# Block sums for the first FFN product: another order of the steps on the vector and activation engines

## The chip, the cores and the metric

One core of a Trainium2 chip runs the whole kernel. The metric is device microseconds of one execution, best told by the median of several runs. Engines: PE (matmul, TensorE), PEld (its weight load), DVE (VectorE), ACT (ScalarE), POOL (GpSimd) and SP, whose queue issues most DMAs. Each engine works through its own queue in order.

## The reference, cut to what matters

The block ends in a SwiGLU feed-forward network on 1024 tokens with 1024 features and DFF = 2816:

```python
h2 = rmsnorm(x, norm2_g[l]) * (1.0 + sc2) + sh2
fg, fu = jnp.split(h2 @ w_ffn_in[l], 2, axis=-1)
x = x + gt2 * ((jax.nn.silu(fg) * fu) @ w_ffn_out[l])
return rmsnorm(x, final_g)
```

The change concerns the first lines: the modulated norm `h2`, and the start of the product `h2 @ w_ffn_in`.

## The kernel before, in words

**Numbers.** Every float32 matmul is made of three matmuls on split operands. `split` (L155) writes the high part with an ACT copy (`split_hi`, L152) and the low part with a DVE subtract; `mm3` (L197) then issues high weight by high activation, high by low, low by high. A product of four 128-row tiles (128 x 512 outputs) is 12 matmuls. Where a helper records an operation, the profile gives the helper's line: nearly everything below stands under L107 or L119, so the rows are read by their tile names.

**The product.** The first FFN product is done in blocks with seven products instead of eight (`Pair`, L1144). The activations (1024 features x 1024 tokens, feature tiles in partitions) are a 2 x 2 matrix of blocks, each of KH = 4 tiles of 128 x 512: A11 (tiles 0 to 3, first half of the tokens), A12 (tiles 4 to 7, first half), A21 and A22 (second half). Sums of blocks are needed: S1 = A21 + A22, S2 = S1 - A11 (reached by two subtractions in place, L1268 and L1269), S4 = A12 - S2, S3 = A11 - A21 (in place of A21). On the weight side T1 = B12 - B11, T2 = B22 - T1, T3 = B22 - B12, T4 = B21 - T2 (`source`, L1167). `PRODUCTS` (L1146) lists the seven products with the PSUM bank (X, Y or Z) that each adds to: 0 is A11 x B11, 1 is S1 x T1, 2 is S2 x T2, 3 is S4 x B22, 4 is S3 x T3, 5 is A12 x B21, 6 is A22 x T4. `evacuate(p)` (L1216) takes what is complete out of a bank: products 0, 1 and 2 are kept by an ACT copy (`kepta`, `keptc`, `keptb`), the others end in a DVE add, and Silu on ACT for a gate pair or a DVE multiply for an up pair. Pairs alternate: even ones are gate columns, odd ones up columns, and there are NFF = 22 of them.

**Order.** `order` (L1243) begins with the first two pairs (one gate, one up) side by side, because the sums of activation blocks are being made meanwhile: product 0 of both, then 5, 1, 2, 3, 4 and 6 of both, 14 products, numbered n = 0 to 13. Then come 20 pairs with products 0 to 6 each. In the loop at L1292 step n first makes the block sums in `before[n]` (L1284), then prepares the weight block of step n + LEAD (LEAD = 6; `prepare`, L1178: a DVE subtract for a T block, then ACT high, DVE low), then issues the product and its evacuation. Ten weight blocks rotate (`weight_block`, L1247). The raw weights of a pair are loaded by `load` (L1155) through SP, into the buffers that an earlier pair frees with its T3 and T4.

**Norm and sums.** `Norm2` (L1060) has the second half of the tokens as `norms[1]`. `stat` (L1077) sums squares on PE and makes the reciprocal root on ACT (Ln, a table load, Exp); it comes after product 0 of the first pair. `apply` (L1084) scales a tile on DVE (L1087) and adds the shift on ACT (L1088). `apply1(j)` (L1258) applies the norm to tiles j and 4 + j, adds the two and splits the sum into S1. `sums` (L1265) makes S2, `sum4` (L1272) S4, and two lambdas S3 and A22, each through `act_block` (L1099), which is a split.

**Queues.** From L1280 on `in_order(True, (T, V, A))` chains the instructions of PE, DVE and ACT: each of these engines executes them in the order in which the program emits them. DMA issues on SP and POOL are not chained.

**Slots.** The four-kilobyte tiles come from 32 slots. Four S3 tiles, two hidden tiles and four A22 tiles reuse slots that become free as the sums before them are done.

Of the kernel before, what the change touches and what calls it, by code (L numbers as in the profile page):

```python
# [10 lines left out]
F32 = mybir.dt.float32  # L11
F32R = mybir.dt.float32r
AF = mybir.ActivationFunctionType
ALU = mybir.AluOpType
# [5 lines left out]
KD = D // P  # L20
KH = KD // 2
# [5 lines left out]
NFF = DFF // P  # L27
# [3 lines left out]
HB = 512  # L31
# [40 lines left out]
LEAD = 6  # L72
# [21 lines left out]
def tile_hybrid_block(ctx: ExitStack, tc: tile.TileContext, xT, vecs, cvec, lamv, relb, bsel, bmask, jrev,  # L94
# [27 lines left out]
    V, A, T, G = Engine(nc.vector), Engine(nc.scalar), Engine(nc.tensor), nc.gpsimd  # L122
# [42 lines left out]
    class Weights:  # L165
# [77 lines left out]
    def col(g, k):  # L243
        return cols[:, g * KD + k:g * KD + k + 1]
# [86 lines left out]

    small = const.tile([P, 16], F32, name="small")
    eps, eps64, heps, nlam, g08 = (small[:, i:i + 1] for i in range(5))
    G.memset(eps, EPS)
    G.memset(eps64, EPS * 2.0 ** -64)
    G.memset(heps, EPS * 2.0 ** -3)
# [27 lines left out]
    with tc.tile_pool(name="psS", bufs=2, space=bass.MemoryType.PSUM) as psS, \  # L364
# [54 lines left out]
        with tc.tile_pool(name="st", bufs=2) as st:  # L419
# [61 lines left out]
            for k in range(KD):  # L481
# [3 lines left out]
                if k in KS:  # L485
                    j = KS.index(k)
# [101 lines left out]
        for j in range(2):  # L588
# [7 lines left out]
                        op0=ALU.mult)  # L596
# [192 lines left out]
        class Norm:  # L789
# [105 lines left out]
    with tc.tile_pool(name="ps2", bufs=6, space=bass.MemoryType.PSUM) as ps2, ExitStack() as fxs:  # L895
# [69 lines left out]
        stages = dict(zip(CN, (cn.means, cn.center, squares, cn.scales, cn.finish)))  # L965
# [42 lines left out]
        for m in range(0, KD, 2):  # L1008
            i = [j[1] for j in jobs].index(m + 1) + 1
# [29 lines left out]
        x1 = []  # L1039
# [20 lines left out]
        class Norm2:  # L1060
# [20 lines left out]
                    T.matmul(st, ones, self.sq, start=False, stop=True)  # L1081
                self.r = rstd_from([st], 1.0 / D, self.last)[0]

            def apply(self, m):  # L1084

                x = x1[m][:, self.hs]
                V.scalar_tensor_tensor(out=x, in0=x, scalar=col(4, m), in1=self.r, op0=ALU.mult, op1=ALU.mult)  # L1087
                A.activation(x, x, AF.Identity, bias=col(3, m))  # L1088

        norms = [Norm2(hf) for hf in range(2)]  # L1090
        x1_d = dp.tile([KD, P, S], F32, name="x1_d")
        g_d = dp.tile([NFF, P, S], F32, name="g_d")
        acts = {}
# [50 lines left out]
        class Pair:  # L1144
# [31 lines left out]
                return b[name]  # L1176

            def prepare(self, p):  # L1178
                name = self.PRODUCTS[p][1]
                src = self.source(name)  # L1180
                w = weight_block()
                split(w[:, :HB], w[:, HB:], src)
                self.w[name] = w

            def product(self, p):
                an, bn, x = self.PRODUCTS[p]
                first = x not in self.banks
                if first:
                    self.banks[x] = bank("f" + x.lower())
                w = self.w[bn]  # L1190
                for k, a in enumerate(acts[an]):
                    ks = slice(k * P, (k + 1) * P)
                    ls = slice(HB + k * P, HB + (k + 1) * P)

                    mm3(self.banks[x], w[:, ks], w[:, ls], a[:, :HB], a[:, HB:], first and k == 0, k == KH - 1,
                        skip_group_check=not first)
# [44 lines left out]
        pairs = [Pair(i) for i in range(NFF)]  # L1241
# [5 lines left out]
        def weight_block():  # L1247
            n = nblock[0] % NWB
            nblock[0] += 1
            if n < NWB - 4:  # L1250
                return fx[0].tile([P, D], F32R, tag="wb", name="wb", bufs=NWB - 4)
            return wp.tile([P, D], F32R, tag="whi" if n % 2 else "wlo", name="wbp")
# [2 lines left out]
            if n < len(order):  # L1255
                order[n][0].prepare(order[n][1])

        def apply1(j):  # L1258
            for m in (j, KH + j):
                norms[1].apply(m)  # L1260
            t = t2("s1")
            V.tensor_tensor(out=t, in0=x1[j][:, HB:], in1=x1[KH + j][:, HB:], op=ALU.add)
            act_block("S1", j, t)

        def sums(j):  # L1265

            a11, a21, a22 = x1[j][:, :HB], x1[j][:, HB:], x1[KH + j][:, HB:]
            V.tensor_tensor(out=a21, in0=a11, in1=a21, op=ALU.subtract)  # L1268
            V.tensor_tensor(out=a11, in0=a22, in1=a21, op=ALU.subtract)  # L1269
            act_block("S2", j, a11)  # L1270

        def sum4(j):  # L1272
            a12 = x1[KH + j][:, :HB]
            V.tensor_tensor(out=a12, in0=a12, in1=x1[j][:, :HB], op=ALU.subtract)
            act_block("S4", j, a12)

        jobs += [(oc, m, Weights(w_oc[m:m + 2], D, f"oc{m}")) for m in range(0, KD, 2)]
        jobs.extend((wo, i, Weights(w_out[i % KD], D, f"wo{i}")) for i in range(2 * KD))
# [1 line left out]
        in_order(True, (T, V, A))  # L1280
        for m in range(WA[KD], KD):
            apply0(m)
        js = range(KH)
        before = {2: [(apply1, 0), (apply1, 1)], 3: [(apply1, 2)],  # L1284
                  4: [(apply1, 3)] + [(sums, j) for j in js],
                  6: [(sum4, j) for j in js],
                  8: [(lambda j: act_block("S3", j, x1[j][:, HB:]), j) for j in js],
                  10: [(lambda j: act_block("A22", j, x1[KH + j][:, HB:]), j) for j in js]}

        late = {}  # L1290
        G0 = list(range(NFF - 6, NFF))
        for n, (g, p) in enumerate(order):  # L1292
            for f, j in before.get(n, ()):
                f(j)
            nxt = n - 5 if n in (7, 8) else g.i + 2 if n >= 14 and p == 1 else NFF
            if nxt < NFF:
                pairs[nxt].load()
            prepare(n + LEAD)
            for f in late.get(n - len(order), ()):
                f()  # L1300
            g.product(p)
            if n == 0:
                norms[1].stat()
# [26 lines left out]
        x1 = []  # L1330
        for gi, grp in enumerate(groups):
            n = len(grp)
# [146 lines left out]
```

## Time and profile before

| | us |
|---|---|
| median of 3 runs | 1434.23 |
| lowest and highest | 1432.81 and 1439.95 |
| the profiled execution, its own time | 1435.16 |
| its span in the profile | 1433.4 |

In that execution PE is busy 96% of the span, DVE 69%, ACT 42%, and the mean granted PE clock is 0.979. Times of rows are microseconds from the span's start; a timeline row has start, duration, engine, line, operation, output<-input and a count, and in brackets the idle time before it with the releaser. A row with x4 is four instructions merged, and its duration runs from the first start to the last end.

### The profile page before, as it was taken

The page shows a single profiled execution, that of the slowest core. Times are in us where ns is not written, and L with a number is a line of the kernel's source. Part 1 is how long each engine was busy: PE and PEld are TensorE (multiplying, and loading weights), DVE is VectorE, ACT ScalarE, POOL GpSimd, SP SyncE. Part 2 cuts the span into 40 slices and gives each one's busy share as a digit, 9 for nine tenths or more (in the row PEclk, how much of TensorE's full clock was granted, in tenths as well). Part 3 has the DMA queues.
Part 4 walks back from the last instruction along what each step waited for, and adds up shares of the span by engine and source line. Part 5 has one row for each costly group of instructions (what it writes and reads, how often), then busy time and mean ns, then how long its engine had stood idle before and what let it go on. Part 6 is the DMA issues. An engine that isn't in the chain of part 4 may idle for free.

```text
span 1433.4 us, 16115 instructions
## 1 busy us (share of the span) xinstructions
PE 1374.6 (96%) x6178; PEld 1120.9 (78%) x6178; DVE 983.6 (69%) x1587; ACT 599.4 (42%) x974; POOL 72.1 (5%) x84
## 2 busy tenths in 40 slices
PE   7799999999999999999977999999999999999996
PEld 4578887878788887887744888888888888888886
DVE  6947688899989896897867556666555554434345
ACT  4436667666511115533654333333333342202145
POOL 3400000000000000000100000000000000000004
PEclk9999999999999999999978999999999999999998
DMA  7601010101111123259501233332222334413203
GB/s 274 202 20 45 30 43 17 45 15 30 45 59 44 44 89 109 85 205 336 162 15 59 88 118 118 106 112 79 86 88 88 110 126 176 136 51 103 77 16 118
DMA packets 44271, 135.11 MB, mean 94 GB/s; under 512 B 4857, under 2 KB 7841, under 8 KB 44194
## 3 DMA queue, kind: packets, MB, share of 16 engines
q1 hardware_dynamic: 39458, 118.88, 25.0%
q0 software_dynamic: 4160, 14.68, 3.0%
q8 instruction: 48, 0.79, 0.2%
q10 hardware_dynamic: 576, 0.52, 0.1%
q14 instruction: 29, 0.24, 0.1%
HBM read 115.19 MB, written 18.88 MB: 94 GB/s over the span
## 4 chain that ended last, share of the span: by engine, by line
PE 81%; DVE 9%; ACT 6%; DMA 1%; issue 1%; POOL 1%; SPq 0%; DVEq 0%; ACTq 0%; POOLq 0%
PE fx L107 16%; PE fo L119 16%; PE proj L107 9%; PE fz L107 8%; PE gc L107 6%; PE ga L107 5%; PE fy L107 4%; PE wo L119 4%; PE oc L119 3%; PE oa L107 3%; PE sc L107 2%; DVE adac L119 2%; PE av L107 2%; PE wps L107 1%; PE vacc L119 1%
## 5 line engine op out<-in xcount | busy, mean ns | idle before, releaser
L119 DVE SCALAR_TENSOR_TENSOR x1r<-fo,cols,x1r 128x512 f32<-128x512 f32 (+1 forms) x72 | 49.3, 690 | 119.8 <-PE fo L119 119.5
L119 PE MATMUL fo<-gl,wh_fo 128*128 128x512 f32 x288 | 112.2, 389 | 0.0
L119 PE MATMUL fo<-gh,wl_fo 128*128 128x512 f32 x288 | 112.1, 389 | 0.0
L119 PE MATMUL fo<-gh,wh_fo 128*128 128x512 f32 x288 | 111.9, 389 | 0.0
L107 DVE SCALAR_TENSOR_TENSOR cacc<-u,vec,cacc 128x1022 f32<-128x1022 f32 (+28 forms) x87 | 110.2, 1267 | 2.2
L107 PE MATMUL proj<-hhi,wh_in 128*128 128x512 f32 x239 | 98.8, 413 | 1.7 <-DVE kl L119 1.7
L107 PE MATMUL proj<-hhi,wl_in 128*128 128x512 f32 x240 | 94.4, 393 | 0.0
L107 PE MATMUL proj<-hlo,wh_in 128*128 128x512 f32 x240 | 94.1, 392 | 0.0
L107 PE MATMUL fz<-S,wb 128*128 128x512 f32 x312 | 80.4, 405 | 10.6 <-ACT S L107 10.4
L107 PE MATMUL fx<-A,wb 128*128 128x512 f32 x335 | 82.0, 401 | 5.2 <-DVE g L107 5.2
L107 PEld LDWEIGHTS fz<-S,wb 128*128 128x128 f32 x312 | 60.4, 195 | 26.5 <-ACT S L107 12.2
L107 PEld LDWEIGHTS fx<-A,wb 128*128 128x128 f32 x335 | 64.9, 194 | 19.7 <-issue 6.0
L119 ACT ACTIVATE wh_fo<-wr_fo 128x768 fp32r<-128x768 f32 x24 | 20.3, 846 | 135.2 <-PE fo L119 129.7
L107 PE MATMUL fx<-S,wb 128*128 128x512 f32 x312 | 74.8, 389 | 0.0
L107 DVE TENSOR_TENSOR wb<-tt,wb 128x512 fp32r<-128x512 f32 x52 | 36.0, 693 | 49.8 <-ACT wb L107 49.8
L107 PEld LDWEIGHTS fx<-S,wb 128*128 128x128 f32 x312 | 58.6, 188 | 12.2
L119 PEld LDWEIGHTS fo<-gl,wh_fo 128*128 128x128 f32 x288 | 54.1, 188 | 11.7 <-DVE gl L119 0.4
L119 PEld LDWEIGHTS fo<-gh,wl_fo 128*128 128x128 f32 x288 | 54.1, 188 | 11.3
L119 PEld LDWEIGHTS fo<-gh,wh_fo 128*128 128x128 f32 x288 | 54.1, 188 | 11.2
L107 ACT ACTIVATE wb<-tt 128x512 fp32r<-128x512 f32 x52 | 32.7, 629 | 63.1 <-DVE tt L107 62.9
L107 PE MATMUL fz<-S,wbp 128*128 128x512 f32 x216 | 56.5, 409 | 2.4 <-ACT S L107 1.7
L119 ACT ACTIVATE e<-sc,mn 128x512 f32<-128x512 f32 (+7 forms) x64 | 47.2, 740 | 26.0 <-DVE mn L119 25.1
(332 smaller groups left out, 3418.2 us busy)
## 6 DMA issues: line engine op xcount, KB each, us to landing
ada<-in_w_ada SPq DMA_DIRECT2D x32, 512.0 KB, 4.4
rawu<-in_w_fi SPq DMA_DIRECT2D x22, 512.0 KB, 3.6
rawg<-in_w_fi SPq DMA_DIRECT2D x22, 512.0 KB, 4.3
g_d<-g POOLq DMA_DIRECT2D x20, 512.0 KB, 4.2
gl<-g_d SPq DMA_DIRECT2D x20, 512.0 KB, 6.0
wr_fo<-in_w_fo SPq DMA_DIRECT2D x24, 384.0 KB, 3.2
adac<-in_w_ada SPq DMA_DIRECT2D x16, 512.0 KB, 4.4
wr_wo<-in_w_out SPq DMA_DIRECT2D x16, 512.0 KB, 5.1
```

Of the source, the lines that this page charges most:

```text
L107: self.last = f(*args, **kw)
L119: self.last = self.chain(f, *args, **kw) if self.chain else f(*args, **kw)
```

## The change

Five things are altered. (1) S1 is formed from the scaled tiles before the shift, and the sum of the two shift columns (`bsum`, four columns made once) is added as the bias of the ACT high part and inside the DVE low part; the shifts of the tiles follow on ACT. (2) The high and low part of a block are separate functions that `staged` emits step by step. (3) Products 1, 2 and 3 of the first two pairs are issued tile by tile, in turn for the two pairs. (4) Weight splits of the first steps are made two at a time by `both`: 6 and 7 ahead of product 0, 8 and 9 after the statistic, 10 to 13 after S4, 14 and 15 after A22, 16 after product 6. (5) The first 14 steps are written out; evacuations move behind the block sums; from n = 14 the loop prepares up to two blocks a step until it is again six ahead.

```diff
+    bsum = small[:, 12:12 + KH]
...
-            def apply(self, m):
+            def scale(self, m):
 
                 x = x1[m][:, self.hs]
                 V.scalar_tensor_tensor(out=x, in0=x, scalar=col(4, m), in1=self.r, op0=ALU.mult, op1=ALU.mult)
+
+            def shift(self, m):
+                x = x1[m][:, self.hs]
                 A.activation(x, x, AF.Identity, bias=col(3, m))
...
+            def high(self, p):
                 name = self.PRODUCTS[p][1]
                 src = self.source(name)
-                w = weight_block()
-                split(w[:, :HB], w[:, HB:], src)
-                self.w[name] = w
-
-            def product(self, p):
+                w = self.w[name] = weight_block()
+                split_hi(w[:, :HB], src)
+                return w, src
+
+            def low(self, part):
+                w, src = part
+                V.tensor_tensor(out=w[:, HB:], in0=src, in1=w[:, :HB].bitcast(F32), op=ALU.subtract)
+
+            def product(self, p, part=range(KH)):
...
+        def both(*ns):
+
+            parts = [(order[n][0], order[n][0].high(order[n][1])) for n in ns]
+            for g, part in parts:
+                g.low(part)
+
+        def staged(*stages):
+
+            for i in range(KH + len(stages) - 1):
+                for k, f in reversed(list(enumerate(stages))):
+                    if 0 <= i - k < KH:
+                        f(i - k)
...
+        def scale1(j):
+
             for m in (j, KH + j):
-                norms[1].apply(m)
-            t = t2("s1")
+                norms[1].scale(m)
+            acts["S1"][j] = slot(f"S1_{j}", F32R)
+            t = sums1[j] = t2("s1")
             V.tensor_tensor(out=t, in0=x1[j][:, HB:], in1=x1[KH + j][:, HB:], op=ALU.add)
-            act_block("S1", j, t)
+            A.activation(acts["S1"][j][:, :HB], t, AF.Identity, bias=bsum[:, j:j + 1])
+            for m in (j, KH + j):
+                norms[1].shift(m)
+
+        def low1(j):
+            t = acts["S1"][j]
+            V.scalar_tensor_tensor(out=t[:, HB:], in0=sums1[j], scalar=bsum[:, j:j + 1],
+                                   in1=t[:, :HB].bitcast(F32), op0=ALU.add, op1=ALU.subtract)
...
+        def blocks(name, get):
+            new_block(name)
+            staged(lambda j: high(name, j, get(j)), lambda j: low(name, j, get(j)))
...
-        js = range(KH)
-        before = {2: [(apply1, 0), (apply1, 1)], 3: [(apply1, 2)],
-                  4: [(apply1, 3)] + [(sums, j) for j in js],
-                  6: [(sum4, j) for j in js],
-                  8: [(lambda j: act_block("S3", j, x1[j][:, HB:]), j) for j in js],
-                  10: [(lambda j: act_block("A22", j, x1[KH + j][:, HB:]), j) for j in js]}
+
+        two = pairs[:2]
+        V.tensor_tensor(out=bsum, in0=cols[:, 3 * KD:3 * KD + KH], in1=cols[:, 3 * KD + KH:4 * KD], op=ALU.add)
+
+        def products(p):
+            for k in range(KH):
+                for g in two:
+                    g.product(p, (k,))
...
+        both(6, 7)
+        two[0].product(0)
+        norms[1].stat()
+        both(8, 9)
+        two[1].product(0)
+        new_block("S1")
+        for g in two:
+            g.product(5)
+        staged(scale1, low1)
+        evacuations(0)
+        products(1)
+        evacuations(5)
+        new_block("S2")
+        staged(sums, lambda j: low("S2", j, x1[j][:, :HB]))
+        evacuations(1)
+        products(2)
+        new_block("S4")
+        staged(sum4, lambda j: low("S4", j, x1[KH + j][:, :HB]))
+        evacuations(2)
+        products(3)
+        both(10, 11)
+        both(12, 13)
+        pairs[2].load()
+        pairs[3].load()
+        blocks("S3", lambda j: x1[j][:, HB:])
+        evacuations(3)
+        for g in two:
+            g.product(4)
+        blocks("A22", lambda j: x1[KH + j][:, HB:])
+        both(14, 15)
+        evacuations(4)
+        for g in two:
+            g.product(6)
+        both(16)
+        evacuations(6)
+        nprep = 17
...
         for n, (g, p) in enumerate(order):
...
+            if n < 14:
+                continue
+            if p == 1 and g.i + 2 < NFF:
+                pairs[g.i + 2].load()
+            for _ in range(2):
+                if nprep <= n + LEAD:
+                    prepare(nprep)
+                    nprep += 1
```

`evacuations(p)` calls `evacuate(p)` for both pairs. `high(name, j, src)` and `low(name, j, src)` are the two halves of `act_block`.

## Rows read from the trace of the kernel before

**Rows 1.** The page, part 1: busy time of each engine.

```profile
PE 1374.6 (96%) x6178; PEld 1120.9 (78%) x6178; DVE 983.6 (69%) x1587; ACT 599.4 (42%) x974; POOL 72.1 (5%) x84
```

**Rows 2.** The chain that ended last, in order of time: start, duration, engine, tile.

```profile
719.80 2.49 PE fx L107 x11
...
787.75 11.22 PE fx L107 x36
798.97 2.72 PE fz L107 x12
...
1177.05 222.21 PE fo L119 x996
```

**Rows 3.** What PE waited for, 690 to 840 us: total, times, longest.

```profile
PE fz L107 <- ACT S L107: 12.1, 7, 4.2
PE fx L107 <- DVE g L107: 5.2, 1, 5.2
```

**Rows 4.** Busy time by stretch; after POOL's column stands the granted PE clock.

```profile
740.00:750.00 10.00, 4.30 (x8) 2.42 (x9) 7.28 (x11) 3.57 (x7) 0.00 (x0) 0.50 0.00 0
```

**Rows 5.** The same in stretches of 2 us, at the restart of PE.

```profile
787.00:789.00 2.00, 1.25 (x3) 1.09 (x4) 0.79 (x3) 1.15 (x2) 0.00 (x0) 0.50 0.00 0
...
793.00:795.00 2.00, 2.00 (x9) 1.64 (x8) 0.60 (x1) 1.12 (x2) 0.00 (x0) 0.84 0.94 344
```

**Rows 6.** Timeline of DVE.

```profile
728.33 1.41 DVE L107 SCALAR_TENSOR_TENSOR x<-x,cols,rstd 128x512 f32<-128x512 f32 x2
730.53 0.69 DVE L107 TENSOR_TENSOR s<-x,x 128x512 f32<-128x512 f32 x1 [0.79 <-ACT x L107]
731.92 0.69 DVE L107 TENSOR_TENSOR S<-s,S 128x512 fp32r<-128x512 f32 x1 [0.70 <-ACT S L107]
732.53 1.41 DVE L107 SCALAR_TENSOR_TENSOR x<-x,cols,rstd 128x512 f32<-128x512 f32 x2
...
748.23 0.68 DVE L107 TENSOR_TENSOR x<-x 128x512 f32<-128x512 f32 x1
748.95 0.69 DVE L107 TENSOR_TENSOR x<-x,x 128x512 f32<-128x512 f32 x1
...
750.95 0.68 DVE L107 TENSOR_TENSOR x<-x 128x512 f32<-128x512 f32 x1
...
759.10 0.69 DVE L107 TENSOR_TENSOR tt<-rawg 128x512 f32<-128x512 f32 x1
...
763.07 0.68 DVE L107 TENSOR_TENSOR x<-x,x 128x512 f32<-128x512 f32 x1
...
765.06 0.69 DVE L107 TENSOR_TENSOR x<-x,x 128x512 f32<-128x512 f32 x1
...
775.40 2.50 DVE L107 TENSOR_TENSOR S<-x,S 128x512 fp32r<-128x512 f32 x4 [0.31 <-ACT S L107]
...
786.92 0.68 DVE L107 TENSOR_TENSOR g<-fx,keptc 128x512 f32<-128x512 f32 x1
```

**Rows 7.** Timeline of ACT.

```profile
727.07 0.62 ACT L107 ACTIVATE wbp<-tt 128x512 fp32r<-128x512 f32 x1
...
729.11 1.39 ACT L107 ACTIVATE x<-x,cols 128x512 f32<-128x512 f32 x2 [0.94 <-DVE x L107]
731.25 0.63 ACT L107 ACTIVATE S<-s 128x512 fp32r<-128x512 f32 x1 [0.76 <-DVE s L107]
...
736.62 1.28 ACT L107 ACT_TABLE_LOAD   x1
738.04 0.63 ACT L107 ACTIVATE g<-g 128x512 f32<-128x512 f32 x1
...
774.75 2.18 ACT L107 ACTIVATE S<-x 128x512 fp32r<-128x512 f32 x4
```

**Rows 8.** Timeline of SP: issue of a raw weight tile of the third pair.

```profile
771.74 0.33 SPq L1162 DMA_DIRECT2D rawg<-in_w_fi  x1
```

**Rows 9.** The page, part 6: KB each, median us from issue to landing.

```profile
rawg<-in_w_fi SPq DMA_DIRECT2D x22, 512.0 KB, 4.3
```

More of the change, by code (lines that the diff above doesn't have):

```diff
@@ L1082, in stat, with apply @@
                 self.r = rstd_from([st], 1.0 / D, self.last)[0]
-            def apply(self, m):
+            def scale(self, m):
                 x = x1[m][:, self.hs]
                 V.scalar_tensor_tensor(out=x, in0=x, scalar=col(4, m), in1=self.r, op0=ALU.mult, op1=ALU.mult)
+            def shift(self, m):
+                x = x1[m][:, self.hs]
                 A.activation(x, x, AF.Identity, bias=col(3, m))
+            def apply(self, m):
+                self.scale(m)
+                self.shift(m)
         norms = [Norm2(hf) for hf in range(2)]
@@ L1178, in prepare @@
             def prepare(self, p):
+                self.low(self.high(p))
+            def high(self, p):
                 name = self.PRODUCTS[p][1]
                 src = self.source(name)
-                w = weight_block()
-                split(w[:, :HB], w[:, HB:], src)
-                self.w[name] = w
-            def product(self, p):
+                w = self.w[name] = weight_block()
[5 more added lines that the diff above has]
+            def product(self, p, part=range(KH)):
                 an, bn, x = self.PRODUCTS[p]
-                first = x not in self.banks
-                if first:
+                if part[0] == 0:
+                    self.first = x not in self.banks
+                first = self.first
+                if first and part[0] == 0:
                     self.banks[x] = bank("f" + x.lower())
                 w = self.w[bn]
-                for k, a in enumerate(acts[an]):
+                for k in part:
+                    a = acts[an][k]
                     ks = slice(k * P, (k + 1) * P)
@@ L1256, in prepare, with new_block, high, low @@
                 order[n][0].prepare(order[n][1])
-        def apply1(j):
+        def both(*ns):
[7 more added lines that the diff above has]
+                        f(i - k)
+        def new_block(name):
+            acts[name] = [None] * KH
+        sums1 = {}
+        def scale1(j):
             for m in (j, KH + j):
-                norms[1].apply(m)
-            t = t2("s1")
+                norms[1].scale(m)
+            acts["S1"][j] = slot(f"S1_{j}", F32R)
+            t = sums1[j] = t2("s1")
             V.tensor_tensor(out=t, in0=x1[j][:, HB:], in1=x1[KH + j][:, HB:], op=ALU.add)
-            act_block("S1", j, t)
+            A.activation(acts["S1"][j][:, :HB], t, AF.Identity, bias=bsum[:, j:j + 1])
[5 more added lines that the diff above has]
+                                   in1=t[:, :HB].bitcast(F32), op0=ALU.add, op1=ALU.subtract)
+        def high(name, j, src):
+            t = acts[name][j] = slot(f"{name}_{j}", F32R)
+            split_hi(t[:, :HB], src)
+        def low(name, j, src):
+            t = acts[name][j]
+            V.tensor_tensor(out=t[:, HB:], in0=src, in1=t[:, :HB].bitcast(F32), op=ALU.subtract)
         def sums(j):
@@ L1269, in sums @@
             V.tensor_tensor(out=a11, in0=a22, in1=a21, op=ALU.subtract)
-            act_block("S2", j, a11)
+            high("S2", j, a11)
         def sum4(j):
@@ L1274, in sum4 @@
             V.tensor_tensor(out=a12, in0=a12, in1=x1[j][:, :HB], op=ALU.subtract)
-            act_block("S4", j, a12)
+            high("S4", j, a12)
+        def blocks(name, get):
+            new_block(name)
+            staged(lambda j: high(name, j, get(j)), lambda j: low(name, j, get(j)))
         jobs += [(oc, m, Weights(w_oc[m:m + 2], D, f"oc{m}")) for m in range(0, KD, 2)]
@@ L1282, in tile_hybrid_block, with evacuations @@
             apply0(m)
-        js = range(KH)
-        before = {2: [(apply1, 0), (apply1, 1)], 3: [(apply1, 2)],
-                  4: [(apply1, 3)] + [(sums, j) for j in js],
-                  6: [(sum4, j) for j in js],
-                  8: [(lambda j: act_block("S3", j, x1[j][:, HB:]), j) for j in js],
-                  10: [(lambda j: act_block("A22", j, x1[KH + j][:, HB:]), j) for j in js]}
+        two = pairs[:2]
[4 more added lines that the diff above has]
+                    g.product(p, (k,))
+        def evacuations(p):
+            for g in two:
+                g.evacuate(p)
+        both(6, 7)
[29 more added lines that the diff above has]
+        evacuations(4)
+        for g in two:
+            g.product(6)
+        both(16)
+        evacuations(6)
+        nprep = 17
         late = {}
@@ L1292, in tile_hybrid_block @@
         for n, (g, p) in enumerate(order):
[L1293 to L1298, printed above, removed]
+            if n < 14:
[6 more added lines that the diff above has]
+                    nprep += 1
             for f in late.get(n - len(order), ()):
@@ L1301, in tile_hybrid_block @@
             g.product(p)
-            if n == 0:
-                norms[1].stat()
             g.evacuate(p)
```

## The prediction

> **What bounds the kernel now.** I read the page's busy times first: PE is busy 96% of the span [rows 1], so a change gains only where PE stands still or runs slowly. Then the chain that ended last, in order of time. Around 720 us it enters the products of the first pairs, and one product of 12 matmuls takes 2.72 us at the full clock. The first two pairs begin at 719.8, and the first product of the third pair ends at 798.97; after that the chain is PE alone up to the second FFN product and through it [rows 2]. So what is gained before 799 stays to the end: nothing behind it waits for anything but PE. Between these two marks lie 15 products, 15 x 2.72 = 40.8 us of work in 79.2 us. Some 38 us are lost there, and that is all this change can reach.
>
> What loses them? PE's waits name the high parts of the sums on ACT, 12.1 us on bank Z, and one wait of 5.2 us for DVE at the end [rows 3]. These waits hide a second loss: with PE half idle the granted clock is 0.50, the lower level, 1.2 GHz [rows 4], and after the wait that ended at 787.75 it is at 0.50 again, and within 793 to 795 it is back on its way up [rows 5]. The 36 matmuls from 787.75 took 11.22 us where three products take 8.16 [rows 2]: 3.06 us given to the clock.
>
> Behind the waits stand two queues that wait for each other. In one round of S1 DVE scales two tiles, waits 0.79 us for ACT's shift, adds, waits 0.70 for ACT's high part, and makes the low part: 4.20 us from 728.33 to 732.53 [rows 6]. A round of S2 (two dependent subtractions, high, low) takes 748.23 to 750.95 = 2.72 us, a round of S4 763.07 to 765.06 = 1.99 us [rows 6]. Without a wait, DVE issues every 0.60 us (four in 2.50, one lasts 0.69) [rows 6], and ACT every 0.52 (four in 2.18) [rows 7]. The end of this chain is the subtraction for S-, then A-blocks, then `g<-fx,keptc` at 786.92, which frees bank X: PE starts product 6 when it ends, at 787.75 [rows 2, 6].
>
> **The change part by part.** `staged` walks its stages in reversed order: in step i it emits the last stage for tile i-1 and then the first for tile i. With two stages the sequence is first(0), last(0), first(1), last(1): no skew at all, the same sequence as a plain loop. DVE is chained, so the low part still stands right behind its own high part and still waits for ACT. I therefore keep ACT's latency in every round, and count by the DVE queue from its first scale at 728.33 [rows 6].
>
> *Ahead of the sums.* Splits 6 and 7 are made before the statistic, 8 and 9 after it, in place of one split and the two keeps. ACT gets one more high part (0.62, [rows 7]) ahead of the last square; DVE has two low parts instead of one ahead of the first scale. That extra high part may be hidden (PE still has product 0 to do) or cost its whole time; one low part replaces the wait for it. Bounds 0.1 and 0.7; I take 0.4, between them, since the square stands nearly at PE's need. First scale 728.7.
>
> *S1.* Two scales end 1.41 us after they start; the add waits some 0.04 (as the second subtraction at 748.95 does behind the first) and lasts 0.69; 0.03 later ACT begins a high part that now carries a bias, as a shift does (two in 1.39 [rows 7], so 0.7); 0.04 later the low part, and the next scale some 0.66 after that. Sum 1.41 + 0.04 + 0.69 + 0.03 + 0.7 + 0.04 + 0.66 = 3.57 against 4.20 [rows 6]. The shifts lie beside it on ACT. Four rounds 14.3: 743.0.
>
> *Evacuation 5, now behind S1.* Its three DVE operations wait: behind the last high part ACT has two shifts (1.39), two keeps (1.15), the table load for Silu (1.28) and Silu itself (0.63) [rows 7] before the up pair's multiply, some 4.5 us, less what the low part covers, plus the multiply's 0.6: 4.3 us on DVE, where three operations take 1.8. Before, the table load at 736.62 lay beside DVE work [rows 7]. Bounds 1.8 (all hidden) and 4.9; I take 4.3. Now 747.3, only 0.9 ahead of 748.23 [rows 6].
>
> In the row, the next activation starts 1.42 us after the table load begins, and it had also waited for its input [rows 7]. The Trainium skill, "ScalarE: Activation LUTs", section "What ACT_TABLE_LOAD costs", counts a drain of about 1.38 us beside the load, 2.66 in all for each switch. By that the sum would lose about 1.3 us more; the row leaves no room for it behind the load.
>
> *S2 and S4.* Unchanged rounds: 4 x 2.72 = 10.9 (758.2) and 4 x 1.99 = 8.0 (766.2). But the two T3 blocks that stood between them, 759.10 to 763.07 [rows 6], move behind S4, to the T4 blocks.
>
> *Splits 10 to 13.* Two at a time the wait for ACT is nearly covered by the other block: eight DVE operations, 4.8 + 0.4 = 5.2 us where four single blocks cost 4 x 1.99 = 8.0. 771.4. This is a true gain of 2.8.
>
> *S3, evacuation 3, A22, splits 14 and 15, evacuation 4.* 2.4 (four low parts at 0.60; the highs run ahead) + 2.0 (one add, Silu beside the second add, multiply) + 2.4 + 2.0 (one subtraction, its high, two lows) = 8.8: 780.2. Splits of the third pair need its raw weights; their issue follows T4 (before at 771.74, [rows 8]), now about 769.5, landing 4.3 us later [rows 9], ahead of their use at 776 to 778. Then `g<-fx,keptc`, 0.68, and PE 0.15 later: product 6 starts at 781.0 instead of 787.75 [rows 2, 6]. **First term: 6.7 us.**
>
> *PE.* Products 1 to 3 tile by tile in turn: 6 matmuls per tile, 1.36 us at full clock, under each round (3.57, 2.72, 1.99), so PE follows DVE, and only the last tile's matmuls remain behind it. After S4 PE idles until S3 exists, about 766.5 to 772, and will restart at the lower clock, as it did at 787.75, for some 6 us. Product 4 of both pairs, 24 matmuls, then takes 13 x 0.45 + 11 x 0.23 = 8.4 us (the lower clock doubles 2.72/12) and ends near 780.4, just when DVE frees bank X. So product 6 starts with hardly a gap, at the full clock, and the 3.06 us of the old restart do not come back. **Second term: 3.0 us.** The half-clock part of product 4 is covered by DVE's work; without this cover it would cost the same 3.
>
> *After it.* At n = 14 only three blocks are ahead, not six. Block 17 is made right behind evacuation 6, about 790.5; PE needs it at 786.5 + 3 x 2.72 = 794.7. Then two blocks a step, some 3.3 us of DVE beside 2.72 of PE, for three steps; the margin of 4 us covers the difference. Cost nothing; uncovered, about 2 us a block.
>
> **Sum:** 6.7 + 3.0 = 9.7 us. The profiled execution took 1435.16 with a span of 1433.4; it would be 1425.5. The median of the runs, 1434.23, lies 0.9 below the profiled one, so I forecast 1424.5.
>
> **The rivals.**
> (a) *The clock falls again.* If PE's gap before product 6 is longer, or product 4 starts at another moment, product 6 runs at 1.2 GHz as at 787.75 [rows 5]. For it: clock and gaps of [rows 4, 5]. Against: a gap under 1 us. It takes back the second term: 1434.2 - 6.6 = 1427.6.
> (b) *The lead of three blocks is too short.* Two or three late blocks at 2 us: gain 4 to 5.5, 1429.5. Against: the margin of 4 us.
> (c) *The table switch costs as the page has it*, a drain on the path behind S1: gain 8.4, 1425.8. Against: [rows 7].
> (d) *The steps really are skewed*, if the engines' order were not the emitted one. DVE would lose its waits: about 0.9 a round in S1, 0.8 in S2 and S4 each, at most 10 us; PE's own work would take back some 2.5. 1417. Against: the rows show act, wait and low in the emitted order [rows 6].
> (e) *Slower.* Splits 14 and 15 stand ahead of evacuation 4 on DVE, and their high parts ahead of Silu on ACT. If the third pair's raw weights land late, bank X is not freed and PE stands. It decides from a landing 10 us past 776, that is 16 us after the issue instead of 4.3 [rows 9]; at 24 us the kernel is 8 us slower, 1442. Against it: every load of that row's median.
>
> **How the numbers follow.** Forecast 0.62, (a) 0.17, (b) 0.08, (c) 0.04, (d) 0.05, (e) 0.04. 0.5% is 7.2 us, about what a measurement of this kernel can tell from no change. Faster by more: the forecast, (c) and (d), and of (a) the third whose sum comes out over 7.2 us: 0.76. Within: the rest of (a), and (b): 0.20. Slower: 0.04. The bounds of the unknowns (0.3 ahead of the sums either way, +2.5 and -0.6 at evacuation 5) put the forecast at 1421.5 to 1425.5; (a), (b) and (c) reach up to 1429.5 or so, and half a microsecond is left for the scatter: 1421 to 1430, which leaves out (d), (e) and the tail of (b).
>
> **What would show it.** Right: first scale near 728.7; rounds of S1 at 3.6, of S2 at 2.7, of S4 at 2.0 with a DVE wait for the high part in each; a stall of DVE of over 2 us between S1 and S2 with a table load in it; no weight blocks between S2 and S4; `g<-fx,keptc` near 780; product 6 at full clock; one product each 2.72 us from there. Wrong: DVE busy through S2 and S4 without waits (d), a granted clock of 0.50 in product 6 (a), PE waiting for weight blocks after 787 (b), or for raw weights (e).

## The result and the profile after

| | before | changed |
|---|---|---|
| median, us | 1434.14 (4 runs, 1432.81 to 1439.95) | 1425.15 (4 runs, 1424.41 to 1426.24) |
| span of the profiled execution, us | 1433.4 | 1423.3 |
| mean granted PE clock | 0.979 | 0.986 |

The ratio is 0.993, with a 95% interval of 0.9902 to 0.9958: faster by 0.7%, 9 us. The forecast was 1424.5, in a range of 1421 to 1430.

Where the time came from shows in one stretch, measured the same way in every run below: from the first matmul of product 0 to the end of the third pair's first product. Before, it begins here (timeline of PE, kernel before):

```profile
719.41 0.39 PE L104 MATMUL fx<-A,wb 128*128 128x512 f32 x1
```

It ends at 798.97 [rows 2], so it lasts 79.56 us. Product 6 begins 68.34 us into it, and the 36 matmuls of product 6 of both pairs and the third pair's first product take 11.22. The same views of the changed kernel, first PE's timeline:

```profile
718.87 0.39 PE L104 MATMUL fx<-A,wb 128*128 128x512 f32 x1
...
748.90 7.69 PE L107 MATMUL fx<-S,wbp 128*128 128x512 f32 x18 [4.63 <-ACT S L107]
...
770.72 8.28 PE L107 MATMUL fx<-S,wb 128*128 128x512 f32 x24 [3.54 <-ACT S L107]
780.66 8.42 PE L107 MATMUL fx<-A,wb 128*128 128x512 f32 x36 [1.66 <-DVE g L107]
```

and its chain that ended last:

```profile
789.09 2.72 PE fz L107 x12
```

The stretch is 789.09 - 718.87 = 70.22 us, 9.34 less than before. Product 6 begins 61.79 us into it: 6.55 of the gain. Its 36 matmuls, answering to the row at 787.75 in [rows 2], take 8.42 instead of 11.22: 2.80 of the gain. Of the 10.1 us by which the spans differ, 0.54 lies ahead of the first product (718.87 against 719.41), and 0.2 behind the stretch. The 0.54 is scatter and no gain: in the profiles below the first matmul begins anywhere from 717.85 to 721.54.

What PE waited for in 690 to 840 us, answering to [rows 3]:

```profile
PE fx L107 <- ACT S L107: 8.6, 3, 4.6
PE fz L107 <- ACT S L107: 4.3, 3, 1.4
PE fz L107 <- DVE S L107: 1.8, 7, 0.3
PE fx L107 <- DVE g L107: 1.7, 1, 1.7
```

The kernel before has one more large row for the sums, which [rows 3] does not show:

```profile
PE fx L107 <- ACT S L107: 1.9, 2, 1.3
```

With two small ones (0.9 and 0.5 us) PE waited 15.4 us for the sums before, and 14.9 after: about as much. What shrank is the wait for `g` at the end, from 5.2 to 1.7 us; the rest of the 9.34 us is matmuls that ran in less time, 2.80 of it in the 36 named above. DVE's timeline of the changed kernel, answering to [rows 6]:

```profile
728.18 1.41 DVE L107 SCALAR_TENSOR_TENSOR x<-x,cols,rstd 128x512 f32<-128x512 f32 x2
729.62 0.69 DVE L107 TENSOR_TENSOR s<-x,x 128x512 f32<-128x512 f32 x1
731.11 0.75 DVE L107 SCALAR_TENSOR_TENSOR S<-s,small,S 128x512 fp32r<-128x512 f32 x1 [0.80 <-ACT S L107]
731.78 1.41 DVE L107 SCALAR_TENSOR_TENSOR x<-x,cols,rstd 128x512 f32<-128x512 f32 x2
...
742.03 0.75 DVE L107 SCALAR_TENSOR_TENSOR S<-s,small,S 128x512 fp32r<-128x512 f32 x1 [0.79 <-ACT S L107]
743.74 0.69 DVE L107 TENSOR_TENSOR g<-fy,kepta 128x512 f32<-128x512 f32 x1 [0.96 <-ACT kepta L107]
744.34 0.68 DVE L107 TENSOR_TENSOR kepta<-fy,kepta 128x512 f32<-128x512 f32 x1
746.16 0.69 DVE L107 TENSOR_TENSOR g<-kepta,g 128x512 f32<-128x512 f32 x1 [1.14 <-ACT g L107]
746.77 0.68 DVE L107 TENSOR_TENSOR x<-x 128x512 f32<-128x512 f32 x1
...
757.63 0.69 DVE L107 TENSOR_TENSOR x<-x,x 128x512 f32<-128x512 f32 x1
...
765.60 0.69 DVE L107 TENSOR_TENSOR tt<-rawg 128x512 f32<-128x512 f32 x1
...
770.79 2.49 DVE L107 TENSOR_TENSOR S<-x,S 128x512 fp32r<-128x512 f32 x4
...
779.83 0.68 DVE L107 TENSOR_TENSOR g<-fx,keptc 128x512 f32<-128x512 f32 x1
...
781.83 0.68 DVE L107 TENSOR_TENSOR tt<-rawg,tt 128x512 f32<-128x512 f32 x1
```

The column to read is the starts: S1 from 728.18, evacuation 5 from 743.74 with two waits, S2 from 746.77, S4 from 757.63, the weight blocks from 765.60, S3 from 770.79, and bank X free after 779.83. For the weight blocks five more rows of the kernel before are needed (timeline of DVE):

```profile
736.72 0.68 DVE L107 TENSOR_TENSOR wbp<-rawg,wbp 128x512 fp32r<-128x512 f32 x1
...
742.12 0.68 DVE L107 TENSOR_TENSOR wbp<-rawu,wbp 128x512 fp32r<-128x512 f32 x1
...
771.03 0.68 DVE L107 TENSOR_TENSOR tt<-rawg,tt 128x512 f32<-128x512 f32 x1
...
784.93 0.68 DVE L107 TENSOR_TENSOR tt<-rawg,tt 128x512 f32<-128x512 f32 x1
786.31 0.69 DVE L107 TENSOR_TENSOR wbp<-tt,wbp 128x512 fp32r<-128x512 f32 x1 [0.69 <-ACT wbp L107]
```

From the first scale to `g<-fx,keptc` DVE's path took 58.59 us before and 51.65 after, 6.94 less: 1.31 in S1 with evacuation 5, nothing in S2 and S4, 3.15 in blocks 10 to 13, and 2.48 from S3 on. Part of that is work which left the path. Before, the low parts of blocks 8 and 9 stood between the rounds of S1 (736.72 and 742.12, 0.60 us of DVE's queue each), and block 16 stood ahead of `g<-fx,keptc` (784.93 to 786.92, 1.99 us). In the changed kernel 8 and 9 are made ahead of S1, and block 16 behind evacuation 4 (from 781.83).

ACT's timeline of the changed kernel, answering to [rows 7]:

```profile
741.90 1.32 ACT L107 ACTIVATE x<-x,cols 128x512 f32<-128x512 f32 x2
743.13 1.06 ACT L107 ACTIVATE kepta<-fx 128x512 f32<-128x512 f32 x2
744.21 1.28 ACT L107 ACT_TABLE_LOAD   x1
745.50 0.63 ACT L107 ACTIVATE g<-g 128x512 f32<-128x512 f32 x1
```

Two shifts, two keeps, the table load and Silu stand in a row here, and DVE waits for the keeps (0.96 us) and for Silu (1.14 us).

### The profile page after: what moved, and what is told of

It is laid out like the page before. It is cut to its first block, busy times and chain, and to the rows that moved or that the text cites. A ratio compares the mean times of both kernels' runs of the same rounds, so it can differ in the third digit from the quotient of the medians.

```text
span 1423.3 us, 16124 instructions
## 1 busy us (share of the span) xinstructions
PE 1365.6 (96%) x6178; PEld 1114.0 (78%) x6178; DVE 982.9 (69%) x1588; ACT 599.3 (42%) x974; POOL 72.0 (5%) x84
## 4 chain that ended last, share of the span: by engine, by line
PE 79%; DVE 10%; ACT 6%; DMA 3%; issue 1%; POOL 1%; SPq 0%; DVEq 0%; ACTq 0%; POOLq 0%
PE fx L107 16%; PE fo L119 16%; PE proj L107 8%; PE fz L107 8%; PE gc L107 6%; PE ga L107 5%; PE fy L107 4%; PE oc L119 3%; PE oa L107 3%; PE wo L119 2%; PE sc L107 2%; DVE adac L119 2%; PE av L107 2%; DMA ada<-in_w_ada 1%; DMA wr_wo<-in_w_out 1%
## 5 line engine op out<-in xcount | busy, mean ns | idle before, releaser
L107 PE MATMUL fz<-S,wb 128*128 128x512 f32 x312 | 76.5, 391 | 5.1 <-ACT S L107 4.3
L107 PE MATMUL fx<-S,wbp 128*128 128x512 f32 x216 | 55.7, 408 | 5.3 <-ACT S L107 5.1
```

The costliest lines, as they stand in the source:

```text
L107: self.last = f(*args, **kw)
```

## The experiments

All were profiled and timed beside the kernel before. The table has, from each profile: the start of product 6 counted from the first matmul, PE's wait just ahead of it, the time of the 36 matmuls from there, and the stretch; then the median and the ratio to before with its interval (to runs of before on the same chip, with medians of 1433.8 to 1435.0). The first four columns are of one profiled execution each. The first of them holds some scatter: where the order ahead of S1 is that of the changed kernel, the first scale stands 9.03 to 9.31 us behind the first matmul, so differences below 0.3 us say nothing of DVE's path. Two kernels are told apart by their times only where the intervals of their ratios do not overlap.

| kernel | product 6 at | wait ahead | 36 matmuls | stretch | median | ratio |
|---|---|---|---|---|---|---|
| before | 68.34 | 5.16 | 11.22 | 79.56 | 1434.14 | 1 |
| changed | 61.79 | 1.66 | 8.42 | 70.22 | 1425.15 | 0.993 [0.9902, 0.9958] |
| forward order | 52.49 | 3.59 | 9.92 | 62.41 | 1418.76 | 0.9896 [0.9882, 0.991] |
| blocks one at a time | 64.90 | 1.72 | 8.42 | 73.32 | 1428.78 | 0.9968 [0.9956, 0.998] |
| products by pair | 61.71 | 3.61 | 9.90 | 71.61 | 1427.78 | 0.9958 [0.9943, 0.9972] |
| before, new S1 alone | 68.19 | 6.10 | 9.84 | 78.03 | 1434.61 | 1.0004 [0.9994, 1.0013] |
| changed, old S1 | 62.60 | 2.17 | 10.07 | 72.67 | 1426.92 | 0.9952 [0.9934, 0.997] |
| ACT's part early | 59.54 | 2.38 | 10.05 | 69.60 | 1423.82 | 0.9915 [0.9901, 0.9929] |
| T3 blocks ahead of S4 | 61.62 | 3.61 | 10.07 | 71.69 | 1426.75 | 0.9945 [0.993, 0.996] |
| before, filler | 68.34 | 1.12 | 8.42 | 76.76 | 1432.66 | 0.9988 [0.9979, 0.9997] |
| changed, filler | 61.50 | 3.63 | 9.83 | 71.33 | 1428.03 | 0.9956 [0.994, 0.9973] |
| evacuation 4 first | 59.59 | 0 | 8.42 | 68.01 | 1423.53 | 0.9925 [0.9908, 0.9942] |
| forward, ACT early | 51.15 | 2.02 | 8.44 | 59.59 | 1415.89 | 0.9863 [0.985, 0.9876] |
| the same, evacuation 4 first | 49.33 | 1.64 | 8.45 | 57.78 | 1412.72 | 0.9852 [0.9828, 0.9876] |

**Is the emitted order skewed?** The stages in forward order:

```diff
-                for k, f in reversed(list(enumerate(stages))):
+                for k, f in enumerate(stages):
```

> The changed kernel with the stages emitted in forward order, so that the first stage of tile i stands ahead of the last stage of tile i-1 on DVE. Theory (the order emitted by the change is the plain one, and DVE loses ACT's latency in every round): the waits of DVE for S's high part vanish, rounds fall from 3.67, 2.71 and 1.99 us to about 2.7, 1.9 and 1.2, DVE reaches g<-fx,keptc some 9 us earlier, PE's own work takes 1 to 3 us of it back: stretch from the first matmul of product 0 to the end of the third pair's first product 62 to 64 us (79.6 before, 70.2 changed), time about 1418. Rival (the changed order is already skewed, the waits lie elsewhere): as the changed kernel, 70 us and 1425.

DVE's waits, total, times and longest, in 727 to 790 us of the kernel before and then in 727 to 785 us of the changed one:

```profile
DVE S L107 <- ACT S L107: 8.7, 13, 0.7
```

```profile
DVE S L107 <- ACT S L107: 8.7, 12, 0.8
```

and all of DVE's waits with the forward order, 728 to 785 us:

```profile
DVE wbp L107 <- ACT wbp L107: 7.1, 4, 5.2
DVE g L107 <- PE fx L107: 4.1, 1, 4.1
DVE g L107 <- ACT g L107: 1.3, 2, 1.1
DVE g L107 <- ACT kepta L107: 1.0, 1, 1.0
```

The change left DVE's 8.7 us of waiting for the sums' high parts as they were; one line removes them all. Product 6 starts 9.3 us earlier than with the change, and the clock takes 1.5 back. The theory held to the microsecond (62.4, 1418.8). The skew that the functions are built for is not in the changed kernel.

**What is making blocks two at a time worth?**

```diff
-            parts = [(order[n][0], order[n][0].high(order[n][1])) for n in ns]
-            for g, part in parts:
-                g.low(part)
+            for n in ns:
+                prepare(n)
```

> The changed kernel with each weight block prepared by itself (subtract, high, low, then the next) instead of two at a time. Theory (blocks in pairs cover ACT's latency): blocks 10 to 13 cost 8.0 us of DVE instead of 5.2, blocks 14 and 15 some 0.6 more, and as the chain of DVE sets the start of product 6, the stretch grows by 3.0 to 4 us to 73.2 to 74.2, time about 1428.5. Rival (weight blocks lie beside other work anyway): 70.2 us, 1425.

Product 6 starts 3.11 us later, the matmuls behind it are untouched, and the stretch is 73.3. From the first scale to `g<-fx,keptc` DVE takes 55.03 us here, 3.38 more than in the changed kernel (the first scale itself stands 0.27 us earlier). The blocks lie on DVE's path, and pairing them is worth 3.1 us of the stretch: a third of the change.

**What are products tile by tile in turn worth?**

```diff
-            for k in range(KH):
-                for g in two:
-                    g.product(p, (k,))
+            for g in two:
+                g.product(p)
```

> The changed kernel with products 1, 2 and 3 issued for one pair and then for the other, instead of tile by tile in turn. Theory (DVE is the bound, PE follows it with time to spare): more of PE's work falls behind the last tile of each sum, 3.4 us at the full clock instead of 1.4, but product 4 waits for S3 anyway: the stretch stays at 70.2 within 0.7 us, time 1425. Rival (PE's work in turn is what brings the gain): 73 us or more, 1428 or more.

PE's timeline of this kernel:

```profile
771.55 0.49 PE L107 MATMUL fx<-S,wb 128*128 128x512 f32 x1 [1.44 <-ACT S L107]
772.36 5.53 PE L107 MATMUL fx<-S,wb 128*128 128x512 f32 x23 [0.31 <-DVE S L107]
781.50 9.90 PE L107 MATMUL fx<-A,wb 128*128 128x512 f32 x36 [3.61 <-DVE g L107]
```

DVE's path is the same (51.65 us from the first scale to `g<-fx,keptc` in both, and product 6 at 61.71 against 61.79), as the theory has it, but the size was missed: the stretch is 1.4 us longer. PE had ended product 3 only 1.44 us before S3 came (3.54 in the changed kernel), did the last 23 matmuls of product 4 in 5.5 us, where the changed kernel took 8.3 for its 24, and so stood 3.61 us instead of 1.66 ahead of product 6, where the clock fell. The granted clock, behind POOL's column, in product 4 and at the start of product 6, first of this kernel, then of the changed one:

```profile
772.40:778.00 5.60, 5.48 (x23) 4.20 (x23) 5.35 (x9) 3.54 (x8) 0.00 (x0) 1.00 0.29 116
782.00:784.00 2.00, 2.00 (x6) 1.55 (x5) 1.29 (x2) 0.63 (x2) 0.54 (x1) 0.50 0.00 0
```

```profile
771.00:775.00 4.00, 3.99 (x9) 2.80 (x10) 3.84 (x7) 2.25 (x5) 0.00 (x0) 0.50 0.58 232
781.00:783.00 2.00, 2.00 (x10) 1.66 (x9) 1.40 (x3) 0.64 (x2) 0.54 (x1) 1.00 0.00 0
```

The levels have changed places: 1.00 is 2.4 GHz, 0.50 is 1.2. The order of products is worth nothing on the path that sets the start of product 6; here it shifted where the clock is low.

**What is the new S1 worth?** Alone in the kernel before (scale both tiles, add, high part with bias, shifts, low part; the rest in the old order):

```diff
             for m in (j, KH + j):
-                norms[1].apply(m)
+                x = x1[m][:, n1.hs]
+                V.scalar_tensor_tensor(out=x, in0=x, scalar=col(4, m), in1=n1.r, op0=ALU.mult, op1=ALU.mult)
...
-            act_block("S1", j, t)
+            A.activation(s[:, :HB], t, AF.Identity, bias=bsum[:, j:j + 1])
+            for m in (j, KH + j):
+                x = x1[m][:, n1.hs]
+                A.activation(x, x, AF.Identity, bias=col(3, m))
+            V.scalar_tensor_tensor(out=s[:, HB:], in0=t, scalar=bsum[:, j:j + 1],
+                                   in1=s[:, :HB].bitcast(F32), op0=ALU.add, op1=ALU.subtract)
```

> The kernel before with one part of the change alone: S1 from the unshifted tiles with the summed shift in the bias, the shifts behind the high part; everything else in its old order. Theory: each of four rounds of S1 loses one wait of DVE for ACT, 4.19 to 3.65 us, so product 6 starts 2.2 us earlier; PE still waits about 5 us ahead of it, so the restart at the low clock stays: stretch 77 to 77.6 us against 79.6, time 1432. Rival (the shorter round is taken up elsewhere, as the shifts now stand between the high part and the next): 79.6 us, 1434.

The theory missed. DVE's timeline of this kernel, and ACT's:

```profile
734.11 1.41 DVE L107 SCALAR_TENSOR_TENSOR x<-x,cols,rstd 128x512 f32<-128x512 f32 x2
735.56 0.69 DVE L107 TENSOR_TENSOR s<-x,x 128x512 f32<-128x512 f32 x1
737.04 0.75 DVE L107 SCALAR_TENSOR_TENSOR S<-s,small,S 128x512 fp32r<-128x512 f32 x1 [0.79 <-ACT S L107]
738.78 0.69 DVE L107 TENSOR_TENSOR wbp<-rawg,wbp 128x512 fp32r<-128x512 f32 x1 [0.99 <-ACT wbp L107]
```

```profile
736.91 1.32 ACT L107 ACTIVATE x<-x,cols 128x512 f32<-128x512 f32 x2
738.14 0.62 ACT L107 ACTIVATE wbp<-rawg 128x512 fp32r<-128x512 f32 x1
```

The rounds did get shorter by half a microsecond, but the two shifts now stand between S1's high part and the next weight block's, so DVE waits 0.99 us for each of two blocks that followed at once before. Product 6 moved by 0.15 us, and the time is unchanged (the 1.4 us that the clock spared in the profiled run do not show in the median). This is the longest wait of the table, yet the 36 matmuls behind it cost less than before: the granted clock is at 0.50 already from 786 to 788, while PE waits until 789.73, and at 0.81 from 792 to 794. The rival's mechanism, a wait on the other side of the shifts, is what happened. The opposite edit, the old S1 in the changed kernel:

```diff
-                norms[1].scale(m)
-            acts["S1"][j] = slot(f"S1_{j}", F32R)
+                norms[1].apply(m)
...
-            A.activation(acts["S1"][j][:, :HB], t, AF.Identity, bias=bsum[:, j:j + 1])
-            for m in (j, KH + j):
-                norms[1].shift(m)
+            high("S1", j, t)
...
+            low("S1", j, sums1[j])
```

> The changed kernel with S1 formed as before the change: shift on ACT first, then the sum, a copy as the high part, a subtraction as the low part. Theory: in the new order nothing stands behind the shifts on ACT that DVE needs, so here the shorter round counts in full: rounds of 4.2 instead of 3.67 us, product 6 starts 2.1 us later, stretch 72.3 us, up to 1.5 more if the clock falls, time 1427 to 1428.5. Rival (as in the old order, where the new S1 alone gained nothing): 70.2 us, 1425.

Here too the theory counted too much: product 6 starts 0.81 us later, not 2.1. The rounds are 4.20 us again, 2.2 more for the four, but ACT has no shifts left behind the last high part, and evacuation 5 loses its first wait (0.96 us) and a little of the second (1.02 instead of 1.14):

```profile
743.23 0.69 DVE L107 TENSOR_TENSOR S<-s,S 128x512 fp32r<-128x512 f32 x1 [0.70 <-ACT S L107]
743.83 0.68 DVE L107 TENSOR_TENSOR g<-fy,kepta 128x512 f32<-128x512 f32 x1
```

(DVE's timeline of this kernel.) The other 1.65 us of its longer stretch are the clock. Counted from the first scale, which stands 0.28 us earlier here, to S2's first subtraction, DVE takes 19.69 us against 18.59. So the new S1 is worth 0.16 us of DVE's path in the old order (19.74 against 19.90) and 1.1 in the new one, of the 2.2 that its rounds save: the rest returns as a wait for what ACT does behind the shifts.

**Does evacuation 5 stand on the path?** Table load and keeps moved into ACT's idle time during S1:

```diff
+            if j == 0:
+                A.preload_act_table_set("silu_and_others")
+            if j == 1:
+                evacuations(0)
...
         staged(scale1, low1)
-        evacuations(0)
```

> The changed kernel with ACT's part of evacuations 0 and 5 made earlier: Silu's table is loaded behind the shifts of S1's first tile, and the two keeps stand behind those of the second. Theory (evacuation 5 stands on DVE's path and waits for ACT): of its two waits, 0.96 and 1.14 us, some 0.2 is left, as ACT idles 1.7 us in each round of S1; DVE reaches g<-fx,keptc 1.9 us earlier, stretch 68.3 us against 70.2, time about 1423.3. Rival (the load delays the next high part, or the wait is covered by later slack): 70.2 us, 1425.

DVE's waits for the keep and for Silu fell from 0.96 and 1.14 us to 0 and under 0.2, and product 6 starts 2.25 us earlier. But PE, which finished product 4 earlier still, stood 2.38 us ahead of it, the clock fell, and the 36 matmuls took 10.05 us: 0.6 us of the stretch is left. The expected 68.3 was missed by 1.3 us. The median is 1.3 us below the changed kernel, its single runs from 1420.07 to 1426.65, and the intervals of the two ratios overlap. The wait was on the path; the clock took most of its removal back in the profiled run.

**Does it matter where the T3 blocks stand?** `both(10, 11)` moved from behind `products(3)` to behind `products(2)`.

> The changed kernel with blocks 10 and 11 made between S2 and S4, where they stood before, still two at a time. Theory (all of this lies in one DVE queue, and only its sum counts): product 6 starts 61.8 us after the first product as in the changed kernel; the clock may come out differently, since product 3 now ends later and product 4 starts sooner behind it: stretch 70.2 us, up to 1.5 more if the clock falls ahead of product 6, time 1425 to 1427. Rival (the move behind S4 is what gains, as sums come before weights): product 6 later by 2 us or more.

As the theory had it: product 6 at 61.62, and the clock 1.65 us dearer behind a wait of 3.61 us. DVE takes 51.64 us from the first scale to `g<-fx,keptc`, against 51.65: of the work that stands ahead of `g<-fx,keptc` either way, only the sum counts for product 6, not the order.

**Is the second term the clock?** The kernel before, with work for PE in its wait of 5.16 us:

```diff
+            if n == 12:
+                fill = bankG("fill")
+                for _ in range(NFILL):
+                    T.matmul(fill, pairs[1].w["T3"][:, :P], acts["A12"][0][:, :HB], start=True, stop=True)
```

> The kernel before with 20 extra matmuls into a bank that nobody reads, ahead of product 6 of the first pair, where PE waits 5.16 us for DVE (their results are not used). Theory (the second term: the clock fell in that wait, and the 36 matmuls behind it took 11.22 us instead of 8.4 for that alone): the filler fits into the wait, DVE is untouched, product 6 starts when it did, and the stretch falls by 2.8 us from 79.6 to 76.8, time about 1431.5. Rival (the 36 matmuls are slow for another reason, as operands or banks): 79.6 us or more, 1434.5.

PE's timeline of this kernel:

```profile
776.67 5.62 PE L108 MATMUL fx<-S,wb 128*128 128x512 f32 x24
782.13 4.70 PE L108 MATMUL fill<-A,wb 128*128 128x512 f32 x20
787.95 8.42 PE L108 MATMUL fx<-A,wb 128*128 128x512 f32 x36 [1.12 <-DVE g L108]
```

Product 6 starts exactly when it did, 68.34, and the 36 matmuls take 8.42 instead of 11.22: 2.80 us, the size of the second term, by nothing but keeping PE at work. The time fell by less than the 3 us expected, and its interval only just excludes no change (0.4 to 3.0 us). And is the low clock in product 4 of the changed kernel on the path? Filler behind product 3 there:

```diff
         products(3)
+        fill = bankG("fill")
+        for _ in range(15):
+            T.matmul(fill, two[1].w["B22"][:, :P], acts["A12"][0][:, :HB], start=True, stop=True)
```

> The changed kernel with 15 extra matmuls behind product 3 into a bank that nobody reads (results not used), so that PE does not idle 3.5 us ahead of product 4. Theory (product 4 is covered by DVE's queue): the clock stays up and product 4 takes 5.5 instead of 8.3 us, but product 6 still starts 61.8 us after the first product; PE stands some 3.5 us ahead of it and the clock may fall there: stretch 70.2 to 71.8 us, time 1425 to 1427, no gain. Rival (the half-clock stretch of product 4 is on the path): 67.5 us, 1422.5.

The last 23 matmuls of product 4 took 5.5 us, product 6 started at 61.50, and the wait ahead of it grew to 3.63 us with the low clock behind it: 71.33. Work done sooner ahead of a wait that DVE sets gained nothing, and in this run lost the clock.

**Toward a better version.** Evacuation 4 ahead of splits 14 and 15, first in the changed kernel:

```diff
-        both(14, 15)
         evacuations(4)
+        both(14, 15)
```

> The changed kernel with evacuation 4 ahead of splits 14 and 15, nothing else. Theory: DVE reaches g<-fx,keptc 2.0 us earlier, at 59.0 us after the first product; PE then ends product 4 at 60.1 and goes on without a gap, 1.5 us earlier than before, at the full clock: stretch 68.8 us against 70.2, time 1423.7. Rival (the splits are late instead): 70.2 us or more.

PE goes from product 4 into product 6 without a wait, at 59.59; 68.01 us, 0.8 better than expected, and 1423.5 (the interval of its ratio overlaps that of the change). DVE's path to `g<-fx,keptc` is 2.01 us shorter. Then the forward order with ACT's part early (the keeps here ahead of the last shifts):

> Forward order of the stages together with an early load of Silu's table (behind the first shifts of S1) and the keeps ahead of the last shifts. Theory: the waits of 0.95 and 1.13 us that the forward order left at evacuation 5 fall to 0.2, DVE is 1.9 us earlier than with the forward order alone, and about 1 us of it reaches the end, since product 4 of both pairs and the clock start to bind: stretch 60.5 to 61.7 us against 62.4, time 1417. Rival (PE is the bound by now): 62.4 us, 1418.8.

Better than expected, 59.59 us: the clock stayed up. And both together:

> Forward order, early table and keeps, and evacuation 4 ahead of splits 14 and 15 on DVE. Theory: in the kernel without the last edit PE had ended product 4 and stood 2.0 us for g<-fx,keptc, behind three operations of the splits; without them ahead of it PE goes on at once: stretch 57.8 us against 59.6, time about 1414. Rival (the splits are then late, and PE waits for block 14 or 17 instead): 59.6 us or more.

57.78 us and 1412.72. The stretch came out as expected, but not in the expected way: PE did not go on at once. The last 23 matmuls of product 4 took 5.50 us, against 7.12 in the kernel without the last edit, and PE still stood 1.64 us ahead of product 6. This kernel is 1.5% faster than the one before (interval 1.2 to 1.7%), more than twice the gain of the change.

## Why the prediction was right

The stretch fell by 9.34 us where the sum had 9.7: 6.55 for a first term of 6.7, and 2.80 for a second of 3.0. Term by term:

*The order of `staged`.* Read from the loop, and shown by the unchanged 8.7 us of waits and by the forward order. Rival (d), the skewed steps, was priced at 17 us of gain; made on purpose it gained 17.2 us of the stretch, 15.7 of the median.

*Ahead of the sums.* The first scale stands 9.31 us behind the first matmul, 8.92 before: 0.39, taken as 0.4. That this middle of two bounds was hit so well is partly luck: in the other kernels with the same order ahead of S1 it was 0.11 to 0.39.

*S1.* Rounds of 3.60 to 3.67 us, forecast 3.57.

*Evacuation 5.* From the last low part's end of issue to S2's first subtraction some 4.1 us, forecast 4.3, between its bounds of 1.8 and 4.9. The early table and keeps show that about 2.2 us of it was waiting. The table switch itself shows in ACT's rows: the keep ends at 744.19, the load begins at 744.21, and Silu, whose input had been ready since 744.43, begins at 745.50, 1.29 us after the load began. The Trainium skill, "ScalarE: Activation LUTs", section "What ACT_TABLE_LOAD costs", has 2.66 us with the drain; the trace has room for the load's 1.28 alone, and so rival (c) falls.

*S2, S4, splits 10 to 13.* 10.86, 7.97 and 5.19 us, forecast 10.9, 8.0 and 5.2; the experiment with single blocks gives 3.1 for all pairing, of which 2.8 had been counted for these four.

*S3 to evacuation 4.* 9.04 us, forecast 8.8. Product 6 at 780.66, forecast 781.0, from a start that was half a microsecond early: counted from the first matmul it came 0.2 us later than forecast.

*The clock.* 2.80 us recovered of the 3.06 counted, as the 36 matmuls take 8.42 us at the full clock and not 8.16; the filler in the kernel before gave the same 2.80 alone. The step was right by a smaller margin than the text made of it: it foresaw a gap of some 0.6 us ahead of product 6, and PE stood 1.66, since counted from the first matmul it restarted on product 4 about 0.7 us earlier than forecast, took 0.1 less for it, and product 6 came 0.2 later. Ten kernels of the table have a longer gap; two of them (1.72 and 2.02 us) kept the full clock, and in the other eight, the one before among them, the 36 matmuls took 9.8 us or more. The changed kernel with the old S1 stood only 0.5 us longer than the changed one and lost the clock. Rival (a) was close, and that it did not come is in part luck.

*After it.* No wait of PE for a weight block or a raw load appears in its waits from 785 to 840: the lead of three blocks sufficed, and (b) and (e) did not occur.

One statement behind the sum was too simple: that the shifts lie beside DVE's work on ACT. They do within S1, but not at its end. Of the 2.2 us that the shorter rounds save, the changed kernel gives half back at evacuation 5, and the old order nearly all at the next weight blocks. The forecast had that loss in its term for evacuation 5 and not in the term for S1, so the sum was right while the credit for the algebra would have been wrong.

So the 6.94 us of DVE's path come from 3.4 for pairing blocks and 1.1 for the new S1, both shown by undoing them, and from 3.2 for blocks 8, 9 and 16, which left the path; against this stands the wait for Silu of 1.0 us that evacuation 5 has even with the old S1, and 0.3 is left over. The 3.2 is read from the rows: no run undoes that move alone, though taking splits 14 and 15 off the same path gave 2.0. The forecast's sum holds this part without naming it as a gain.

## What to carry to other kernels

Where two engines hand one tile back and forth in order, write down the emitted sequence of a "pipelined" helper for its first three steps: with the last stage ahead of the first one in each step, two stages are no pipeline, and the waits in the trace (here 8.7 us before and after) tell it at once. Count a chain by the queue of the engine that ends it, and for every operation moved off one wait look for what then stands behind it on the other engine. An engine that finishes sooner ahead of a wait which another one sets gains nothing, and TensorE may pay with the clock behind the wait, as in three profiled runs here.

## What was not expected of the hardware

That work done sooner on PE made the stretch longer: three kernels that brought PE to the wait ahead of product 6 about 2 us earlier (products by pair, T3 blocks ahead of S4, filler behind product 3) had product 6 start within 0.3 us of the changed kernel's, and each took 1.1 to 1.5 us longer over the stretch. In the first of them the rows show product 4 at 2.4 GHz and product 6 begun at 1.2, instead of the reverse; in the other two the granted clock also stands at 1.00 in product 4 and at 0.50 behind the start of product 6 (782 to 784 us, and 780 to 782). This is one profiled run of each. Their ratios, 0.9945 to 0.9958, lean the same way from the 0.993 of the change, but the intervals overlap. In these runs the low level was cheapest where another engine set the pace anyway.
